# Row-wise infinity norm on one core: one 768-column tail load issued as two loads, of 120 and of 8 partitions

## The chip, the cores and the metric

The kernel runs on one core of a Trainium2 chip. The metric is the device time of one execution in microseconds, the median of several executions. Beside it there is one execution taken with the hardware profiler; its span runs from the first to the last instruction that the profile shows.

## The reference

The input x is 8192 x 8192 in float32, 268 MB. The output has one number for each row, the largest absolute value in it:

```python
def reference(x):
    return np.linalg.norm(x, ord=np.inf, axis=1)
```

Each element is read once and goes into one maximum, so the kernel is one long load with a reduction beside it.

## The kernel before

The 8192 rows are spread over 128 partitions, 64 rows to a partition. All loads go into one buffer, `ring`, of three slots of 16384 float32 columns and some padding; every load is issued from SyncE (SP), and every reduction is a `reduce_max` of absolute values on VectorE (DVE), issued by the helper `absmax` (line 255). TensorE and ScalarE compute nothing; ScalarE's queue (ACT) issues two of the three stores.

There are two stages. The bulk stage (line 266) makes 20 loads of two rows per partition, 64 KB per partition and 8 MB in all, each reduced to two maxima by one instruction; the first load's results go to `r_first`, the others' to `r_bulk`. The tail stage handles the last 24 rows of each partition, which lie one behind the other in memory, 196608 columns. They are cut by the list `TAIL` into 37 loads, counted from 0, that get smaller towards the end: from 16384 columns down to 512. Load 31 has 768 columns. A load may hold the end of one row and the start of the next, and a row may be spread over several loads, so each load is cut into pieces at row borders. A piece that ends its row reduces into `r_tail`, over its own columns and the partial maxima of earlier pieces of that row; those were written by VectorE into columns of `ring` just ahead of the last piece. The last 14 loads alternate between two rows.

The order on SP is the order of the program: 20 bulk loads, 37 tail loads (line 297), and at the end the store of `r_tail` (line 318). A load waits for the space in `ring` that it overwrites, and for the completion counter that it uses: there are eight counters for transfers (numbers 99, 100 and 102 to 107 in the trace), taken in turn by all loads and stores, and a transfer is issued only when the one that used the counter before it has landed. Loads 30 to 36 use the counters 103 to 107, 99 and 100. The store of `r_bulk` (line 315, after the reduction of load 34) uses 102, the last store 103. VectorE counts its own instructions on counter 101.

Four functions edit the program once it has been built. `drop_implied_waits` removes waits that another wait already covers, `start_first_load_early` moves the first load to the front, `finish_on_pool` has GpSimd wait for the last stores and reset the counters, and `open_without_vector` leaves VectorE out of the opening barrier.

Of the kernel before, what the change touches and what calls it, by code (L numbers as in the profile page):

```python
# [30 lines left out]
]  # L31


def start_first_load_early(nc):
# [176 lines left out]
@with_exitstack  # L211
def kernel(
    ctx: ExitStack,
    tc: tile.TileContext,
    x: bass.AP,
    out: bass.AP,
    B: int = 2,
    SLOTS: int = 3,
    PAD: int = 128,
):  # L220
    nc = tc.nc
    P = nc.NUM_PARTITIONS
    rows, cols = x.shape
    W = B * cols
    R = SLOTS * W + PAD * 4


    n_tail = sum(w for _, w in TAIL) // cols
    met = 0
    for lo, w in sorted(TAIL):  # L230
        assert lo == met
        met += w
    assert met == n_tail * cols
    n_bulk_rows = rows // P - n_tail
    assert n_bulk_rows % B == 0
    N = n_bulk_rows // B
    split = n_bulk_rows * P
    x_f = x[: P * B].rearrange("(p b) c -> p (b c)", p=P)
    out_f = out[: P * B].rearrange("(p b) -> p b", p=P)
    x_b = x[P * B : split].rearrange("(p n b) c -> n p (b c)", p=P, b=B)  # L240
    out_b = out[P * B : split].rearrange("(p n) -> p n", p=P)
    x_t = x[split:].rearrange("(p t) c -> p (t c)", p=P)
    out_t = out[split:].rearrange("(p t) -> p t", p=P)

    pool = ctx.enter_context(tc.tile_pool(name="sbuf", bufs=1))
    r_first = pool.tile([P, B], F32)
    r_bulk = pool.tile([P, n_bulk_rows - B], F32)
    r_tail = pool.tile([P, n_tail], F32)
    used = [HEAD, B, n_bulk_rows - B, n_tail]
    gap = -sum(-(-n // STEP) * STEP for n in used) % PAD  # L250
    pool.tile([P, gap], F32, name="gap")
    ring = pool.tile([P, R], F32)

    def absmax(o, i):
        return nc.vector.reduce_max(  # L255
            out=o, in_=i, axis=X, apply_absolute_value=True
        )

    def after(ins, first, kind):
        info = mybir.DependencyInfo(kind, mybir.DependencyReason.SCHED_ONLY)  # L260
        tc.add_manual_dep(ins.ins, first.ins.name, info, reason="order")

    for n in range(N):
        at = n % SLOTS * W
        t = ring[:, at : at + W]
        nc.sync.dma_start(out=t, in_=x_f if n == 0 else x_b[n - 1])
        r = r_first[:] if n == 0 else r_bulk[:, (n - 1) * B : n * B]
        absmax(r, t.rearrange("p (b c) -> p b c", b=B))


    pieces = []
    for j, (at, w) in enumerate(TAIL):
        end = at + w
        while at < end:
            r = at // cols
            to = min(end, (r + 1) * cols)
            pieces.append((j, r, to - at))
            at = to
    of_row = [[k for k, s in enumerate(pieces) if s[1] == r] for r in range(n_tail)]


    here = N % SLOTS * W
    start, slot = [], []
    for j, (_, w) in enumerate(TAIL):
        first = next(s for s in pieces if s[0] == j)
        ks = of_row[first[1]]
        n_part = len(ks) - 1 if pieces[ks[-1]][0] == j else 0
        at = -(-(here + n_part) // PAD) * PAD
        if at + w > R:
            at = -(-n_part // PAD) * PAD  # L290
        start.append(at)
        slot.append(at - n_part)
        here = at + w

    for j, (src, w) in enumerate(TAIL):
        at = start[j]
        nc.sync.dma_start(out=ring[:, at : at + w], in_=x_t[:, src : src + w])
        here = [k for k, s in enumerate(pieces) if s[0] == j]
        offs = [at + sum(pieces[i][2] for i in here[:m]) for m in range(len(here))]
        todo = list(zip(here, offs))  # L300
        if slot[j] != at:

            todo = todo[1:] + todo[:1]
        for k, lo in todo:
            _, r, n = pieces[k]
            ks = of_row[r]
            if k == ks[-1]:
                frm = slot[j] if len(ks) > 1 else lo
                done = absmax(r_tail[:, r : r + 1], ring[:, frm : lo + n])
            else:  # L310
                to = slot[pieces[ks[-1]][0]] + ks.index(k)
                done = absmax(ring[:, to : to + 1], ring[:, lo : lo + n])
        if j == len(TAIL) - 3:

            ins = nc.scalar.dma_start(out=out_b, in_=r_bulk[:])
            after(ins, done, mybir.DependencyClass.Sync)
            nc.scalar.dma_start(out=out_f, in_=r_first[:])
    nc.sync.dma_start(out=out_t, in_=r_tail[:])
    nc.at_finalize(drop_implied_waits)
    nc.at_finalize(start_first_load_early)  # L320
    nc.at_finalize(finish_on_pool)
    nc.at_finalize(open_without_vector)
# [30 lines left out]
```

## Time and profile before

| what | value |
|---|---|
| median of 3 executions | 626.89 us (626.55 to 627.07) |
| the profiled execution | 626.98 us |
| its span | 624.3 us |
| VectorE busy | 553.2 us in 76 instructions |
| load queue (q1) | 268.44 MB, 99.6% of 16 channels' span |
| mean rate of transfer | 430 GB/s |

A page of the profile gives busy times and shares of the span, the traffic of each DMA queue, the chain of work that ended last, and the groups of instructions by line with what ended the idle time before them. DVE is VectorE, SP is SyncE, ACT is ScalarE, POOL is GpSimd; SPq and ACTq are rows of issues on those engines. A transfer is carried by 16 DMA engines, called channels here to keep them apart from the compute engines. Beside the page there are views of waits, of the timeline in a stretch, of busy time in windows, and of the instructions that write or read one buffer, with the time from an issue to its landing. The trace also holds each packet of a transfer and each increment of a completion counter with its time, which no view prints one by one. Times of views are microseconds from the start of the span.

### The profile page before, as it was taken

Reading aid. Unit: us, or ns where it says so; the run is one execution under the profiler, and the core shown is the slowest. Engines: PE = TensorE matmul, PEld = TensorE weight load, DVE = VectorE, ACT = ScalarE, POOL = GpSimd, SP = SyncE. Lnnn points to the kernel's source line nnn. Section 1 sums busy time; section 2 is a strip of 40 time slices with the busy share of each in tenths; the row PEclk is TensorE's granted clock in tenths of the full one; section 3 lists DMA queues with packets and bytes.
Section 4 is the critical chain, followed back from the end, with each engine's and each line's share of the span. In section 5 each row is a group of like instructions: output and inputs, shape, how many; then the busy total and the mean of one; then the engine's idle time right before and its main releaser. Section 6 shows DMA issues by size and latency. Waiting matters only on the chain.

```text
span 624.3 us, 168 instructions
## 1 busy us (share of the span) xinstructions
DVE 553.2 (89%) x76; POOL 0.2 (0%) x4
## 2 busy tenths in 40 slices
DVE  0588988889988889888898888988899999999999
POOL 0000000000000000000000000000000000000000
DMA  9999999999999999999999999999999999999998
GB/s 403 470 403 458 416 428 445 403 470 403 470 403 470 403 466 407 458 416 428 445 403 470 403 470 403 470 403 470 392 435 458 408 446 427 421 437 424 431 425 335
DMA packets 8497, 268.47 MB, mean 430 GB/s; under 512 B 1200, under 2 KB 1200, under 8 KB 3120
## 3 DMA queue, kind: packets, MB, share of 16 engines
q1 hardware_dynamic: 8208, 268.44, 99.6%
q10 hardware_dynamic: 288, 0.02, 0.0%
q14 instruction: 1, 0.01, 0.0%
HBM read 268.44 MB, written 0.03 MB: 430 GB/s over the span
## 4 chain that ended last, share of the span: by engine, by line
DMA 61%; DVE 38%; issue 0%; DVEq 0%
DMA ring<-in_x_dram 61%; DVE r_bulk L255 17%; DVE ring L255 10%; DVE r_tail L255 9%; DVE r_first L255 3%; DVEq L348 0%
## 5 line engine op out<-in xcount | busy, mean ns | idle before, releaser
L255 DVE TENSOR_REDUCE r_bulk<-ring 128x2 f32<-128x16384 f32 x19 | 327.2, 17220 | 40.0 <-DMA ring<-in_x_dram 40.0
L255 DVE TENSOR_REDUCE r_tail<-ring 128x1 f32<-128x8192 f32 (+14 forms) x24 | 109.6, 4585 | 7.7 <-DMA ring<-in_x_dram 7.7
L255 DVE TENSOR_REDUCE ring<-ring 128x1 f32<-128x5248 f32 (+26 forms) x32 | 101.4, 3213 | 0.8 <-DMA ring<-in_x_dram 0.8
L255 DVE TENSOR_REDUCE r_first<-ring 128x2 f32<-128x16384 f32 x1 | 17.2, 17219 | 21.9 <-DMA ring<-in_x_dram 21.9
L337 POOL MEMSET const-bfloat16-1.0<- 128x1 bf16 x1 | 0.1, 101 | 0.0
L337 POOL MEMSET const-uint8-127<- 128x1 uint8 x1 | 0.1, 101 | 0.0
L337 POOL MEMSET const-float32-0.0<- 128x1 f32 x1 | 0.1, 98 | 0.2 <-issue 0.2
L337 POOL MEMSET const-float32-1.0<- 128x1 f32 x1 | 0.1, 98 | 0.0
## 6 DMA issues: line engine op xcount, KB each, us to landing
ring<-in_x_dram SPq DMA_DIRECT2D x1, 7744.0 KB, 39.6
ring<-in_x_dram SPq DMA_DIRECT2D x1, 7168.0 KB, 37.2
ring<-in_x_dram SPq DMA_DIRECT2D x1, 6400.0 KB, 32.9
ring<-in_x_dram SPq DMA_DIRECT2D x1, 5696.0 KB, 36.7
ring<-in_x_dram SPq DMA_DIRECT2D x1, 5056.0 KB, 41.0
ring<-in_x_dram SPq DMA_DIRECT2D x1, 4544.0 KB, 36.0
ring<-in_x_dram SPq DMA_DIRECT2D x1, 4032.0 KB, 32.0
ring<-in_x_dram SPq DMA_DIRECT2D x1, 3648.0 KB, 40.3
```

Source lines behind the costliest of these rows:

```text
L255: return nc.vector.reduce_max(out=o, in_=i, axis=X, apply_absolute_value=True)
L337: nc = _bacc.Bacc("TRN2", target_bir_lowering=False, num_devices=1)
```

## The change

A dictionary `CUTS` gives, for a tail load by its number, the partition ranges in which it is issued; a load that is not in it is issued whole. It has one entry: load 31 is issued as a load of partitions 0 to 119 and a load of partitions 120 to 127. Both write the same columns of `ring`, and the one reduction of load 31 reads what both have written. Each of the two takes a completion counter of its own.

```diff
+CUTS = {31: [(0, 120), (120, 128)]}
...
     for j, (src, w) in enumerate(TAIL):
         at = start[j]
-        nc.sync.dma_start(out=ring[:, at : at + w], in_=x_t[:, src : src + w])
+        for lo, hi in CUTS.get(j, [(0, P)]):
+            nc.sync.dma_start(
+                out=ring[lo:hi, at : at + w], in_=x_t[lo:hi, src : src + w]
+            )
```

## The prediction

> **What bounds the kernel now.** I read the page first, then the chain of waits in order of time, the waits of the last stretch, and the issues and landings of single loads. The page:
>
> ```profile
> span 624.3 us, 168 instructions
> DVE 553.2 (89%) x76; POOL 0.2 (0%) x4
> DMA  9999999999999999999999999999999999999998
> q1 hardware_dynamic: 8208, 268.44, 99.6%
> ```
>
> Over the whole span transfers are the limit: the queue that carries the loads (q1) keeps all 16 DMA channels busy for 99.6% of it. But the change touches one load of 3072 bytes per partition out of the last few, so what counts is which engine ends late there. The chain:
>
> ```profile
> 533.56 39.66 DMA ring<-in_x_dram
> 573.22 0.02 issue
> 573.25 10.08 DVE ring L255 x2
> ...
> 606.65 15.18 DVE ring L255 x13
> 621.83 0.45 issue
> 622.28 0.14 DVE r_tail L255
> ```
>
> The last DMA on the chain lands at 573.22 us. From there on it is VectorE alone. The 0.45 us called issue is no idle time: the reduction of 512 columns before it starts at 621.69 and takes 0.674 us, so the next one, at 622.28, begins while it ends. Waits and windows agree:
>
> ```profile
> DVE ring L255 <- DMA ring<-in_x_dram: 0.8, 1, 0.8
> ...
> 573.20:600.00 26.80, 26.75 (x10) 0.00 (x0) 1.00 1.00 426
> 600.00:621.00 21.00, 21.00 (x16) 0.00 (x0) 1.00 1.02 419
> ```
>
> The first row is the only wait of VectorE for a transfer after 571 us: 0.8 us, ended at 573.25. The windows give length, VectorE busy, POOL busy, clock, DMA share, GB/s: VectorE is busy for 21.00 of 21.00 us while the transfers still run at full share. So from 573.25 on both run at their limit, with VectorE just behind the transfers. How far behind is the number this case turns on. Load 31 (the 768 columns that are split), its landing and its reduction:
>
> ```profile
> L297 SPq DMA_DIRECT2D ring<-in_x_dram x1: 328/328/328, 608.5 to 608.5; - x1
> DMA to landing us min/median/max: 10.7/10.7/10.7
> ...
> 619.38 0.94 DVE L255 TENSOR_REDUCE ring<-ring 128x1 f32<-128x768 f32 x1
> ```
>
> Issued at 608.485, landed at 619.204 (the trace's own stamps, finer than the row), reduced from 619.376: it lay there for 0.17 us. For loads 30 to 36 the same subtraction gives 0.24, 0.17, 0.24, 0.17, 0.23, 0.19 and 0.17 us. VectorE never waits for any of them, and nothing that lands earlier than now can start a reduction earlier.
>
> **The change part by part.** The sum is made against the profiled execution: 624.3 us span and 2.7 us outside it, 626.98 us, 0.09 above the median of 626.89.
>
> The pieces on the channels. The trace's packet records show that each load puts 8 rows on each of the 16 channels, every row of load 31 a packet of 0.121 us started every 0.118 us, and a completion packet of about 15 ns more in the spacing. The 16 channels are not level: 15 of them finish load 31 between 617.90 and 618.43, one at 619.20. That one fell back when it also carried a transfer of 8 KB on the instruction queue (q14) at 570.37; before that it was not the last. Every landing since then is set by it, so who gets the rows of load 31 matters only through that channel.
>
> 120 rows and 8 rows are shapes that the trace does not show. Nearest is the load of 128 rows: 8 rows a channel. Taken over, 120 rows are 8 rows on 15 channels, none on one, and the 8 rows go on as few as one or as many as eight channels. Bounds for the late channel: it gets none of load 31 (8 x 0.118 = 0.95 us earlier for loads 32 to 36, then the second latest, 0.78 us earlier, decides) or one row more with its completion packet (0.118 + 0.015 = 0.13 us later). Earlier is worth 0, because VectorE has no wait there to lose. 0.13 us later costs 0 as well, since it is under the smallest margin, 0.17 us, even with the 0.02 us from a landing to the instruction that it releases. If that cover were gone it would cost 0.13 us.
>
> [...]
>
> One more issue on SP. An issue takes 0.328 us, and each of the last loads is issued when the load eight places ahead of it has landed: its completion counter is one of eight taken in turn. The extra load takes one place, so loads 32 to 36 wait for the next landing in line, 1.7, 1.6, 1.4, 1.2 and 1.1 us later than now (the spacing of their issues: 610.33, 612.01, 613.59, 614.99, 616.22, and then the landing of load 29 at 617.30). Behind them on SP only the last store is queued, at 623.59. What covers this is the backlog: load 36 is issued at 616.22 now, and would be at 617.32. From an issue to the first packet the last store takes 0.84 us, so its rows are ready at 618.2; the fastest channel comes to them at 620.47. That leaves 2.3 us, the other loads have more, so the cost is 0. If the backlog were gone each microsecond would count in full.
>
> One more wait on VectorE: the reduction of load 31 needs both counters. A wait standing ahead of a reduction shows twice in the trace (at 621.81 and 622.40), 21 ns each, both while the reduction before is still running; cost 0. Behind it are the reductions of loads 32 to 36, which is why the second piece matters: if it came late, all of them would. The store of the bulk results on ACT waits on a counter that moves one place too, but that landing (618.27) lies 4 us before its issue at 622.39. Cost 0.
>
> Sum: 626.98 + 0 = 626.98, less 0.09 to the median: 626.9 us. Other than zero, terms lie between -0.8 (the whole wait of VectorE that ends at 573.25, if the 8 KB transfer falls elsewhere) and the prices below.
>
> **The rivals.** *The second piece comes in series: slower.* If SP may only issue the 8 rows once the 120 have landed (both write one buffer over the same columns, and the program that places the waits could take them for overlapping), it issues at 619.2 and lands, with the 1.4 us that the 12 KB store takes from issue to landing, at 620.6, 1.3 us after VectorE wants it. Loads 32 to 36, queued behind on SP, start to move at about 620.5 at the earliest and need 0.80 + 0.80 + 3 x 0.65 = 3.55 us on their channels, then 0.33 us to land: 624.4 against the 622.88 at which load 36 is reduced now. That is +1.5 us, 628.4. It decides as soon as the second landing comes over 0.17 us after 619.2. Against it: loads of the same queue lie on the channels back to back (loads 35 and 36 land 0.63 us apart, 8 packets of 0.080 us being 0.64), so no piece pays a latency unless it is made to wait, and the two pieces touch different partitions.
>
> [...]
>
> *The 120 rows fall on fewer channels: slower.* On 8 channels they are 15 rows each, with the extra row 16: (16 - 8) x 0.118 + 0.015 = 0.96 us later on those; if the late channel is one of them, less the 0.17 us margin, +0.8: 627.7. On a single channel 128 rows are 15.1 us instead of 0.95, +14: 641. For it: the trace has no load of other than 128 rows.
>
> *The relief counts: faster.* If the executions without a profile have VectorE waiting in the last loads, where the profiled one does not, up to 0.8 us (the lead of the second latest channel) comes back: 626.1. Against it: the profiled time lies within the three others, 626.55 to 627.07.
>
> *The split does nothing to the balance,* since the rows are dealt evenly over 16 channels whatever the cut: 626.9 as well.
>
> **How the numbers follow.** Nothing on the path, with or without relief of the late channel: 0.66. Relief that counts, 626.1: 0.10. Eight channels, 627.7: 0.09. In series, 628.4: 0.08. One channel, 641: 0.03. Something unseen that is faster: 0.04. A measurement of this kernel tells about 0.2% from no change, 1.25 us; the first three stay inside that, so same is 0.85, slower 0.11, faster 0.04. I take 626.9. The range takes in the first three cases and the spread of the runs around them, 626.0 to 627.9, which leaves 0.15 out.
>
> **What would show it.** Right: VectorE busy without a gap from 573.25 to the end, loads still issued ahead of need, two issues of 360 and 24 KB on SP, the reduction of load 31 starting within 0.1 us of 619.38, and a last reduction near 622.88. If the relief is real, landings of loads 32 to 36 come some 0.7 us earlier and yet the end does not move. Wrong: a wait of VectorE for a transfer after 606 us, an SP issue of the second piece after 619 us, or the last store moved from 623.59 by more than 0.2 us.

## The result and the profile after

The kernel with the cut load takes 628.39 us (median of 11 executions, 628.08 to 628.68) against 626.74 us before in the same series (11 executions). The ratio is 1.0026, 95% interval 1.0016 to 1.0035: slower by 1.65 us, 0.26%. The profiled execution took 628.39 us with a span of 625.7 us.

The load queue moves the same bytes and is as busy as before, over a span that is 1.4 us longer. From the first part of the page (in the kernel after, the helper `absmax` is line 257, L257):

```profile
span 625.7 us, 170 instructions
DVE 553.4 (88%) x76; POOL 0.2 (0%) x4
q1 hardware_dynamic: 8215, 268.44, 99.6%
```

The loss is on the chain of work that ended last. Its last DMA is no longer the one that landed at 573.22 but the one of 8 partitions, issued at 610.03 and landed at 620.62:

```profile
610.03 10.59 DMA ring<-in_x_dram
620.62 0.03 issue
620.65 0.02 DVEq L257
620.67 0.05 issue
620.72 2.46 DVE ring L257 x4
623.18 0.45 issue
```

The timeline of VectorE (start, duration, instruction, idle time before it and what ended it) shows two new waits for transfers. The reduction of load 30, which is not cut, waits 0.75 us, and that of load 31 another 0.70 us:

```profile
606.28 12.03 DVE L257 TENSOR_REDUCE ring<-ring 128x1 f32<-128x1920 f32 x8
619.07 0.95 DVE L257 TENSOR_REDUCE ring<-ring 128x1 f32<-128x768 f32 x1 [0.75 <-DMA ring<-in_x_dram]
620.72 3.00 DVE L257 TENSOR_REDUCE ring<-ring 128x1 f32<-128x768 f32 x4 [0.70 <-DMA ring<-in_x_dram]
623.63 1.29 DVE L257 TENSOR_REDUCE r_tail<-ring 128x1 f32<-128x519 f32 x2
```

After them there is no gap. The last store is issued at 624.95 in place of 623.59, 1.36 us later; since VectorE was 0.29 us earlier than in the profile of before at the reduction of 1920 columns (606.28 against 606.57), the stretch behind it lost 1.65 us. The two waits are 1.45 us of that; the rest is the overlap of some 0.08 us between reductions that follow each other, lost at both waits, and the step over the second counter.

Why a load that is not cut should land late is seen in the windows (length, VectorE busy, POOL busy, clock, DMA share, GB/s). After:

```profile
616.00:617.30 1.30, 1.30 (x3) 0.00 (x0) 1.00 1.03 415
617.30:618.30 1.00, 1.00 (x2) 0.00 (x0) 1.00 1.10 259
618.30:619.30 1.00, 0.25 (x2) 0.00 (x0) 1.00 1.00 212
619.30:620.30 1.00, 0.72 (x1) 0.00 (x0) 1.00 1.03 344
```

and before, in the same stretch (0.3 us later on its clock, for the 0.29 us above):

```profile
617.60:618.60 1.00, 1.00 (x3) 0.00 (x0) 1.00 1.04 412
618.60:619.60 1.00, 1.00 (x2) 0.00 (x0) 1.00 1.05 415
619.60:620.60 1.00, 1.00 (x2) 0.00 (x0) 1.00 1.04 399
```

The share of the DMA engines stays at 1, and the rate falls to half. The channels are not idle: their packets take longer. In the trace's packet records every one of the 256 packets of 3072 bytes took 121 ns before; after, 68 of them took longer, half of these over 195 ns, up to 314. The first slow one starts at 617.33. The first channels had begun the piece of 120 rows some 0.6 us before (their completion packets of load 30 stand from 616.7 on), and the late channel still has rows of load 30 to carry: it lands load 30 at 619.04. The loads behind are slowed even more than load 31: 212 of the 256 packets of loads 32 and 33 took longer than their 102 ns, up to 319. Added up over all channels, the packets of loads 30 and 31 took 5.4 us longer than before and those of loads 32 and 33 11.6 us. So the neighbours on both sides pay as well.

### The profile page after: what moved, and what is told of

Same layout as the page of the kernel before. It is cut to its first block, busy times and chain, and to the rows that moved or that the text cites. A ratio compares the mean times of both kernels' runs of the same rounds, so it can differ in the third digit from the quotient of the medians.

```text
span 625.7 us, 170 instructions
## 1 busy us (share of the span) xinstructions
DVE 553.4 (88%) x76; POOL 0.2 (0%) x4
## 4 chain that ended last, share of the span: by engine, by line
DMA 67%; DVE 32%; DVEq 0%; issue 0%; SPq 0%
DMA ring<-in_x_dram 67%; DVE r_bulk L257 17%; DVE r_tail L257 8%; DVE ring L257 5%; DVE r_first L257 3%; DVEq L353 0%; SPq L300 0%; DVEq L257 0%
## 5 line engine op out<-in xcount | busy, mean ns | idle before, releaser
L257 DVE TENSOR_REDUCE r_bulk<-ring 128x2 f32<-128x16384 f32 x19 | 327.2, 17220 | 40.0 <-DMA ring<-in_x_dram 40.0
L257 DVE TENSOR_REDUCE r_tail<-ring 128x1 f32<-128x8192 f32 (+14 forms) x24 | 109.6, 4586 | 7.7 <-DMA ring<-in_x_dram 7.7
L257 DVE TENSOR_REDUCE ring<-ring 128x1 f32<-128x5248 f32 (+26 forms) x32 | 101.6, 3217 | 1.9 <-DMA ring<-in_x_dram 1.9
L257 DVE TENSOR_REDUCE r_first<-ring 128x2 f32<-128x16384 f32 x1 | 17.2, 17220 | 21.9 <-DMA ring<-in_x_dram 21.9
```

The lines of the kernel that those rows point to most:

```text
L257: return nc.vector.reduce_max(out=o, in_=i, axis=X, apply_absolute_value=True)
```

## The experiments

Theory P: cut like this, the rows are dealt over the channels in another way, channels then get in each other's way at what P calls an entry of the SBUF, the on-chip memory of 128 partitions in which `ring` lies, and each packet slows. P supposes that there are such entries, and it takes the rows of a piece to be dealt in order, so many in a row to each channel. The packet records hold no address, so which rows a channel carries, and where channels meet, is an assumption throughout; no run shows an entry. Rivals: W, the extra issue, the moved counters or the second wait; S, the small load of 8 rows; I, 15 channels in place of 16; F, a fixed cost of a cut; H, the order in which rows are read from HBM (the memory that holds `x`), or the number of rows a channel has.

**Two loads, all partitions.**

```diff
-CUTS = {31: [(0, 120), (120, 128)]}
+CUTS = {31: [(0, 384), (384, 768)]}
...
-                out=ring[lo:hi, at : at + w], in_=x_t[lo:hi, src : src + w]
+                out=ring[:, at + lo : at + hi], in_=x_t[:, src + lo : src + hi]
```

> Load 31 is issued as two loads of all 128 partitions, columns 0 to 383 and 384 to 767: one more issue, one more completion counter taken, two waits ahead of the reduction, as in the change, but each channel keeps its rows. Theory P (the 120 rows are dealt over the channels so that channels meet in the same entry of the SBUF and slow each other): no change, 626.4 to 627.1 us, no VectorE wait for a transfer after 606 us, about 410 GB/s around 618 us. Theory W (the extra issue, the moved counters or the second wait cost the time): about 628.3, as after the change.

Measured: 627.03 us against 626.81, ratio 1.0002 (0.9992 to 1.0011), a span of 624.3 us as before. VectorE runs through, and the rate stands:

```profile
617.30:618.30 1.00, 1.00 (x2) 0.00 (x0) 1.00 1.07 405
618.30:619.30 1.00, 1.00 (x2) 0.00 (x0) 1.00 1.05 416
...
615.13 7.23 DVE L257 TENSOR_REDUCE ring<-ring 128x1 f32<-128x1152 f32 x8
622.28 1.28 DVE L257 TENSOR_REDUCE r_tail<-ring 128x1 f32<-128x519 f32 x2
```

The third line is one run of eight reductions without an idle time, load 31 among them. W falls: one more issue, one more counter and one more wait cost nothing that shows (0.2 us, with an interval of the ratio that spans 1).

**120 rows alone.**

```diff
-CUTS = {31: [(0, 120), (120, 128)]}
+CUTS = {31: [(0, 120)]}
```

> Load 31 loads partitions 0 to 119 only; the last 8 rows are left out, so their maxima are taken over old data. One issue and one counter, as before the change. Theory P: the slow rate stays, under 300 GB/s for about 2 us around 618 us, and the time is 1.0 to 1.6 us above before. Theory S (the small load of 8 rows is what is slow): no change, 626.7. Theory W: no change, 626.7.

Measured: 628.30 us against 626.81, ratio 1.0026 (1.0015 to 1.0037). With one issue, one counter and less data the loss is there. The windows fall to half around the load, though under 300 GB/s for one window of 1 us and not for the 2 us expected:

```profile
617.30:618.30 1.00, 1.00 (x2) 0.00 (x0) 1.00 1.07 364
618.30:619.30 1.00, 0.71 (x1) 0.00 (x0) 1.00 1.02 217
619.30:620.30 1.00, 0.47 (x1) 0.00 (x0) 1.00 1.04 337
```

S and W alone can't be it.

**The 8 rows alone, on top of a whole load.**

```diff
-CUTS = {31: [(0, 120), (120, 128)]}
+CUTS = {}
...
+        if j == 31:
+            nc.sync.dma_start(
+                out=spare[120:128, :], in_=x_t[120:128, src : src + w]
+            )
```

> Load 31 is whole, and the 8 rows of partitions 120 to 127 are loaded a second time into a buffer that nobody reads. Theory P: eight packets on eight channels, all into a few entries, 0 to 0.3 us. Theory S (the small load): 1.2 to 1.6 us above before.

Measured: 627.24 us against 626.81, ratio 1.0006 (0.9996 to 1.0015). VectorE has no wait in the last loads, and the rate stands:

```profile
618.30:619.30 1.00, 1.00 (x2) 0.00 (x0) 1.00 1.04 406
```

All 264 packets of 3072 bytes took 121 ns, the eight of the small piece among them, and only 6 of the 256 of loads 32 and 33 were slowed. The interval reaches from no loss to 0.9 us, so it shuts out S's 1.2 to 1.6 us but does not say whether the small piece costs some tenths.

**112 and 16 rows.**

```diff
-CUTS = {31: [(0, 120), (120, 128)]}
+CUTS = {31: [(0, 112), (112, 128)]}
```

> Load 31 as 112 and 16 partitions. Both numbers divide by 16, so if the rows are dealt evenly every channel carries 7 + 1 rows of it, 8 in all, as before. Theory I (15 channels in place of 16, or eight channels with a ninth row, cost the time): no change, 626.7. Theory P: dealt 7 rows to a channel the rows of different channels still meet in the same entries, 0.6 to 1.6 us above before and a rate under 330 GB/s around 618 us.

Measured: 628.71 us against 626.81, ratio 1.0032 (1.0020 to 1.0044), 1.9 us more and somewhat above what P had allowed. The rate falls, and 73 of the 256 packets of 3072 bytes are slow:

```profile
618.30:619.30 1.00, 0.43 (x1) 0.00 (x0) 1.00 1.02 256
```

Here no channel is left out, since each of the two pieces has 16 increments that come with data, and by an even dealing none has a row more than before. I falls: it isn't how many rows a channel has. That it is which rows is shown by the runs on load 5 below.

**The cut on a large load.**

```diff
-CUTS = {31: [(0, 120), (120, 128)]}
+CUTS = {5: [(0, 120), (120, 128)]}
```

> The same cut, 120 and 8 partitions, is put on load 5 (12800 columns, 50 KB a row, some 15 us of transfer) in place of load 31. Theory P: the loss grows with the bytes of the load; were two channels to share every entry throughout, its 15 us would double, so 8 to 16 us above before, and about half the rate, 215 to 280 GB/s, between some 480 and 505 us. Theory F (a fixed cost of a cut or of 15 channels): at most 1.6 us above before, 628.3.

Measured: 652.33 us against 626.79, ratio 1.041 (1.036 to 1.045): 25.5 us more, well over what P had expected. F falls, but P's price was too low as well. VectorE's waits from 460 us on (us in total, times, longest), before and in this run, show the whole loss in one place:

```profile
DVE r_tail L255 <- DMA ring<-in_x_dram: 1.5, 2, 1.0
```

```profile
DVE r_tail L257 <- DMA ring<-in_x_dram: 27.4, 3, 25.5
```

The packet records say why it is more than a doubling. A row of 51200 bytes takes 1.89 us in the whole load. In the piece of 120 rows most take 4.0 us, and the 8 packets of the small piece 7.9 to 8.6. By these, 8 rows a channel at 4.0 are 32 us and one more at 8.6 makes 40.6; load 5 lies on the channels from 481.36 to 521.49, 40.1 us, where the whole one has 15.6. The small piece is the dearest per byte, with 7.9 to 8.6 us a row against 4.0, and all its eight channels write within eight partitions; that this is the cause is not shown.

The same records show how far the slowing reaches. The channels can be followed one by one here, since each packet starts where the one before it ends, and all fifteen that carry the piece of 120 rows have rows of 4.0 us. The sixteenth channel has no row of load 5 and goes on to load 6: its rows of 45568 bytes take some 3.55 us each, against 1.68 once load 5 is through. While the small piece runs, rows of load 6 on seven other channels take 7.4 to 8.4 us. So in this run the slowing reaches all channels at once, also those that carry no row of the cut load at the time. Why it does is open.

**The same number of rows at two places.** Two kernels load 64 of the 128 rows of load 5. Number of rows, rows per channel, bytes and HBM stride are equal; the partitions differ.

```diff
-CUTS = {31: [(0, 120), (120, 128)]}
+CUTS = {5: [(0, 64)]}
```

> Load 5 loads partitions 0 to 63 only (the other half is left out). [...] Theory H (the order in which HBM rows are read, or the number of rows a channel has, is what is slow): the same picture here as in the run on partitions 32 to 95.

```diff
-CUTS = {31: [(0, 120), (120, 128)]}
+CUTS = {5: [(32, 96)]}
```

> Load 5 loads partitions 32 to 95 only: again 64 rows, 4 to a channel, the same HBM stride, the same size. [...] Theory H: as slow as partitions 0 to 63.

Measured (one execution each): 628.06 us for partitions 0 to 63 and 626.11 us for 32 to 95, against 626.79. In the windows, from 0 to 63:

```profile
485.00:490.00 5.00, 5.00 (x1) 0.00 (x0) 1.00 1.40 287
490.00:495.00 5.00, 5.00 (x2) 0.00 (x0) 1.00 0.85 174
```

and from 32 to 95:

```profile
485.00:490.00 5.00, 5.00 (x1) 0.00 (x0) 1.00 1.09 474
490.00:495.00 5.00, 5.00 (x2) 0.00 (x0) 1.00 1.01 437
```

A packet is booked in these windows as a whole, which is why single ones stand high or low. By the packet records the median row takes 4.01 us in the first and every row 1.89 us in the second, exactly as in the whole load. The load is through in 16.5 us and in 8.2 us. H falls: the number of rows and the strides are equal, and only the place of the rows makes the difference. This is all that P rests on. Place has two meanings here that the runs do not part, because partition p is filled from the same rows of x in every run: where the rows land in the SBUF, and where they lie in HBM. That it is the SBUF is the author's assumption, and no run shows it. A run that loads the rows of partitions 0 to 63 into partitions 32 to 95 would settle it and was not made. The second kernel's time is 0.7 us below before. The first kernel's time is 1.3 us above before: half the data at a bit under half the rate takes 0.9 us longer than the whole.

**Do the times of a row add up?** Two kernels load all of load 5 in pieces. Their sums (rule P) use the two times of a row that the last two runs measured, 1.89 and 4.01 us.

```diff
-CUTS = {31: [(0, 120), (120, 128)]}
+CUTS = {5: [(32, 96), (0, 32), (96, 128)]}
```

> Load 5 in three pieces that together are the whole of it: partitions 32 to 95, then 0 to 31, then 96 to 127. [...] The middle piece has 4 rows a channel, nobody shares: 4 x 1.9 = 7.6 us. Each outer piece has 2 rows a channel, two channels to an entry: 2 x 4.0 = 8.0 us. Together 23.6 us in place of 15.1, so 8 to 9 us above before, 635. If what counts is only that a load is cut, three pieces cost more than two.

Measured: 635.04 us against 627.23, ratio 1.0125 (1.0096 to 1.0155), 7.8 us more, just under the 8 to 9 expected. The load lies on the channels for 23.8 us (481.33 to 505.13). The 64 rows of the middle piece take 1.89 us each, those of the outer ones 3.2 to 4.0.

```diff
-CUTS = {31: [(0, 120), (120, 128)]}
+CUTS = {5: [(0, 64), (64, 128)]}
```

> Load 5 in two halves, partitions 0 to 63 and 64 to 127. Rule P: 4 rows a channel in each half, two channels to an entry all the time: 2 x 4 x 4.0 = 32 us in place of 15.1, 16 to 18 us above before, 643 to 645: twice the loss of the three pieces, with one piece less. If the number of pieces counts, less than the three pieces.

Measured: 644.07 us against 627.23, ratio 1.0269 (1.0236 to 1.0303), 16.8 us more, with 32.1 us on the channels (481.25 to 513.33). VectorE's waits from 460 us on, the three pieces first, then the halves:

```profile
DVE r_tail L257 <- DMA ring<-in_x_dram: 9.8, 3, 8.3
```

```profile
DVE r_tail L257 <- DMA ring<-in_x_dram: 18.2, 3, 16.2
```

23.6 and 32 us had been worked out beforehand. How many channels share an entry, by which those sums chose between 1.9 and 4.0 us for a row, is shown by no run. Shown are 1.89 us a row for partitions 32 to 95, 4.01 for 0 to 63 loaded together, and 3.2 to 4.0 for the outer pieces; for the two halves the 32.1 us on the channels, over 8 rows a channel, give an estimate of 4.0 us a row. Three pieces cost half of what two cost, because the rows of the middle one take 1.89 us as in the whole load; why they do is not shown.

## Why the prediction was wrong

**What bounds the kernel** was read rightly. VectorE runs without a gap from 573.25 on, and each of the last loads lies there for 0.17 to 0.24 us before it is reduced. That margin is also why so small a load can cost anything: a landing that comes a microsecond late is a microsecond lost.

**The pieces on the channels** is the step that failed. It took the price of a row, 0.118 us, from loads of 128 partitions and let only the number of rows per channel vary, so that its bounds were -0.95 and +0.13 us. The trace of before shows 0.118 us only for that one shape. In the trace of after the price itself moves: 68 of the 256 rows of loads 30 and 31 took up to 314 ns, and the loads behind, which the step left at their old price, were slowed as well. On load 5 the same cut made a row 2.1 times as long in the large piece (4.01 over 1.89) and 4.2 to 4.6 times in the small one (7.9 to 8.6 over 1.89). Carried over to load 31, that is an estimate of 8 x 0.25 + 0.5 = 2.5 us on a channel in place of 0.95, some 1.6 us more.

The landings give 1.7 us: the second piece landed at 620.62, and the landing of load 31 before, moved by the 0.29 us that this execution was ahead, is 618.91. That the two agree is in part luck. The late channel landed load 30 at 619.04; before, moved by the same 0.29 us, it was 617.98. So 1.06 us were lost ahead of its rows of load 31, while the other channels were already in loads 31 and 32, and these rows added only 0.65. And eight small rows on top of a whole load had no slow packet among them, so the 0.5 us for one such row is not shown at this size.

The trace of before could not have shown the factor, but the nearest-row bound was no bound: a shape that no load has had could be slower by row, not only by count. The step's 15 ns for a completion packet are 6 ns by the records (8 rows and the packet take 0.947 us), which changes nothing in the sum.

**How many channels** came out as one of the cases that the bounds had taken in, 15 for the 120 rows and eight for the 8. The landings in the trace of after show it: of the 120-row piece's 16 increments one comes 0.5 us after the issue, with no data, and 15 between 618.88 and 620.42; of the small piece's, eight come with data. What was missed was to ask which partitions those channels then write, and whether a row still costs the same there.

**The relief** is real and went to the wrong channel. At load 36 one channel is now 0.35 us ahead of all others (622.29 against 622.64), but the late one is still last, 0.69 us behind the next (623.70 against 623.01). In the small piece, too, one increment comes 1.18 us after the other seven (620.62 against 619.44), so the late channel is among the eight that got a row more.

**One more issue, the moved counters, the second wait** were costed at nothing, and the run with two column halves shows that this was right. The second piece was issued at 610.03 and not held back, as the forecast had it.

**The rivals.** "In series" had given 628.4 us, the measured number, by luck: its mechanism did not happen, with no load issued after 619 us and the pieces landing 0.20 us apart. "Fewer channels" had the right kind of cause, more time on the channels, but a count of rows as its reason, which the cut of 112 and 16 rules out. The two rivals on fewer channels, 0.09 and 0.03, were all that the forecast gave to a shape that the trace had never shown; that was too little. "Relief counts" did not happen, for the reason given.

**The chances.** The forecast of no change stood at 0.85; the loss measured is 0.26%, with an interval from 0.16% to 0.35%, so it is small but clear of zero. The time lies 0.5 us above the upper end of the range, 627.9. Of the signs of being wrong that the forecast named, two came: waits of VectorE for transfers after 606 us, and a last store moved by 1.36 us.

A version that beats both kernels did not come out of these runs. The kernel before is the better one; the 0.8 us that VectorE waits at 573.25 was not gone into.

## What to carry to other kernels

Before a load is cut by partitions, time a row of the pieces at the partitions where they will lie: here a cut that kept every byte and a DMA share of 1 halved the rate, from 415 to 212 GB/s in a window of 1 us, and the loads before and after it shared the loss (5.4 us of packet time on loads 30 and 31, 11.6 us on loads 32 and 33). The cut along the columns kept all 128 partitions in each load and cost nothing that showed (627.03 us against 626.81). In the windows the sign is a DMA share of 1 with a rate that falls (1.00 at 212 GB/s); the share alone hides it.

## What was not expected of the hardware

Rows of 51200 bytes took 1.89 us in the whole load and in the load of partitions 32 to 95, 4.0 us in most of the piece of partitions 0 to 119 and as the median of the load of partitions 0 to 63, and 7.9 to 8.6 us in the piece of 120 to 127, where eight channels write eight neighbouring partitions. Against the whole load that is 2.1 and 4.2 to 4.6 times. What makes the place of a row cost this is not shown.

Channels that carry no row of the cut load slowed as well. During the piece of 120 rows the one channel that carried none of it took 3.55 us for rows of load 6 that otherwise take 1.68, and during the small piece the other channels' rows of load 6 took 7.4 to 8.4 us.
